# Key norms of the recurrence in one chain for four heads instead of two

## The chip, the cores and the metric

The kernel runs on one core of a Trainium2 chip. The metric is the device time of one execution in microseconds (us). TensorE (PE in the profile, PEld for its weight loads) multiplies matrices, VectorE (DVE) and ScalarE (ACT) work element by element, GpSimd (POOL) does small copies and clears, SyncE (SP) issues the transfers. Each engine runs its own instructions strictly in order; semaphores tie the engines together.

## The reference

Two layers, each a token mixer and an MLP, over a sequence of T = 256 tokens with 2048 channels. Half of the mixer is a recurrence of 16 heads with 64 channels each (RWKV-7). What the change touches is the norm of its keys:

```
heads = lambda z: z.reshape(B, T, H, N).astype(jnp.float32)
kk = heads(k * k_k)
kk = kk / jnp.maximum(jnp.sqrt(jnp.sum(kk * kk, -1, keepdims=True)), 1e-12)
k = k * (1 + (a - 1) * k_a)
```

The normalised `kk` enters the state update of every step, beside the receptance `r`, the decay, `k` and the value. The other half of the mixer is an attention of 16 heads; both halves are put together and projected by one output matrix.

## The kernel before

All activations lie with channels on the 128 partitions and the 256 tokens along the free side, so one tile [128, 256] holds two heads, and the recurrence works by such **pairs**: eight pairs per layer, in two halves of four (`half_in(0)`, `half_in(1)`). For pair `p`, `half_in` (L684) makes two blocks of the input projection, first receptance `r`, then key `k`: a block (L240) is 48 matmuls of 128x256 into one PSUM bank `acc`, from two weight units that are loaded (L220), split into a high part `wh` on ACT (L226) and a low part `wl` on DVE (L227). `ev0` (L437) evicts a block through ACT and DVE (L423, L424) into a tile `rk`, of which there are four. In the first half of layer 0 there are no such blocks: `r` and `k` come from sums that are ready before.

Then `rwkv_a` (L491) runs for the pair. It makes two small matmuls `zw`, `za` for decay and gate; from `zw` ACT and DVE make the decay products `P` and `Pi` (L501 to L506); the key's square goes to ACT (L511); `head_rsqrt` (L297) sums it per head and token with two matmuls `tp` of two columns, clamps the sums (L302, 128x4), makes the inverse root in ten DVE instructions of 128x4 (`rsqrt`, L290: one guess at L291, then three rounds of L293, L294, L295), spreads it over the 64 channels (L305, `exa`), turns it with two PE transposes (L308, `rb`) and multiplies it into the key (L514, the normalised key). With it come `bk` (L520 to L522), the two `UR` tiles (L533, L534), sixteen matmuls `mt`, their masks (L541, L542), a transpose `bkt`, `vp`, and `bonus`, whose product with the value (L565, `vt`) ends the pair. All the PSUM tiles of this, `zw`, `za`, `tp`, `rb`, `mt`, `bkt`, `vp`, `bonus`, take turns in one pool of two banks (tag `mxa`), so pairs run one behind the other. When all four pairs of a half are done, `rwkv_b` inverts 32x32 blocks in a long DVE loop, `rwkv_c` runs the state over four chunks, `rwkv_out` finishes (`half_out`). The attention that follows takes its scores (`sc`) from the same two banks.

What sets the order on an engine is a scheduler that places instructions when their inputs are due by its own estimates, earlier code first, with weight splits and evictions raised by `high_priority`. So blocks of later code (attention's inputs `cin`, `Kd`, `q`, and `va`) are laid between the steps of `rwkv_a` on PE, as filler.

Of the kernel before, what the change touches and what calls it, by code (L numbers as in the profile page):

```python
# [15 lines left out]
OP = mybir.AluOpType  # L16
# [151 lines left out]
def tile_trunk(tc, ap, outT, dbg=None):  # L168
    nc = tc.nc
    V, A, G, PE, SY = nc.vector, nc.scalar, nc.gpsimd, nc.tensor, nc.sync  # L170
    with ExitStack() as ctx:
# [4 lines left out]
                "loa": 1, "loc": 1, "sm": 1, "pc": 2, "tya": 6, "tyc": 6, "tyn": 8,}  # L176
# [16 lines left out]
        def tiny(th, n, dt=FT):  # L193
            return st("ty" + th, [128, n], dt)
# [102 lines left out]
        def head_rsqrt(th, sq, ind, floor):  # L297
            tp = mx(th, [128, 2, 2], "tp")
            for i in range(2):
                mm(tp[:, i], sq[:, i * 128:i * 128 + 128], ind)  # L300
            v, y, t = tiny(th, 4), tiny(th, 4), tiny(th, 4)
            V.tensor_scalar(v, tp.rearrange("p a b -> p (a b)"), floor, None, op0=OP.max)  # L302
            rsqrt(y, v, t)
            ex = st("ex" + th, [128, 4, 64])
            V.tensor_copy(ex, y[:, :, None].to_broadcast([128, 4, 64]))  # L305
            b = mx(th, [128, T], "rb")
            for i in range(2):
                PE.transpose(b[:, i * 128:i * 128 + 128], ex[:, 2 * i:2 * i + 2].rearrange("p a b -> p (a b)"), ident)  # L308
            return b
# [100 lines left out]
        for l in range(NL):  # L410
# [80 lines left out]
            def rwkv_a(pi, p, r, k, H):  # L491
# [18 lines left out]
                sq = st("a6", [128, T])  # L510
                A.activation(sq, k, AF.Square, scale=vc(l, "kk", pi))  # L511
                rb = head_rsqrt("a", sq, cs("hind"), 1e-24)
                kkn = st("a7", [128, T])
                V.scalar_tensor_tensor(kkn, k, vc(l, "kk", pi), rb, op0=OP.mult, op1=OP.mult)  # L514
# [9 lines left out]

                V.scalar_tensor_tensor(sq, r, vc(l, "rk", pi), kp, op0=OP.mult, op1=OP.mult)
# [156 lines left out]
            def half_in(half):  # L682
# [3 lines left out]
                for p in range(4):  # L686
                    pi = half * 4 + p
                    for i in range(2):
                        b = 12 + 2 * pi + i
                        if l > 0 or b >= NS:  # L690
                            block(win, 2 * b if half == 0 else 2 * (b + 8), hs, lambda acc: ev0(b, acc))
                        elif b >= 16:
                            ev0(b, sums[b // 2][:, b % 2])
                    rwkv_a(pi, p, rkt.pop(2 * pi), rkt.pop(2 * pi + 1), H)
# [462 lines left out]
```

## Time and profile before

| | us |
|---|---|
| three timed runs, median | 2791.06 (2787.33 to 2794.6) |
| profiled execution, its own time | 2785.48 |
| span of the profiled execution | 2783.7 |
| PE busy / PEld busy | 2657.1 / 2431.0 |
| DVE busy / ACT busy | 2084.5 / 1517.5 |

The profiled execution lies 5.6 us under the median of the runs. Matmuls are pipelined, so a PE that is always busy may still be slow; the busy time of the weight loads (PEld) is the better sign of how well PE is fed, since it fills a stretch only where matmuls follow each other without a wait. The time falls into stretches: layer 0's input start up to 204 us, its mixer up to about 660, its MLP up to 1400, then layer 1's mixer and MLP. The MLPs run at the full rate of matmuls; the mixers don't.

### The profile page before, as it was taken

The numbers are of one execution on the slowest core, as the hardware profiler recorded it, in microseconds if no ns is written. First come the engines' busy times: TensorE is split into PE (matmuls) and PEld (weight loads), VectorE is DVE, ScalarE is ACT, GpSimd is POOL, SyncE is SP. The second block draws the span as 40 slices with busy tenths as digits, with TensorE's granted clock in tenths as the row PEclk, the third lists the DMA queues.
The fourth block names the chain that finished last, engine by engine and source line by source line (L and its number), as shares of the span: only waits on it lengthen the run. The fifth ranks groups of instructions, "written<-read, shape, count | busy, mean of one in ns | idle before, by whom it ended". The sixth has DMA issues, their size and how long they took to land. (4 is left out here: it accounts for less than half of the span.)

```text
span 2783.7 us, 59154 instructions
## 1 busy us (share of the span) xinstructions
PE 2657.1 (95%) x22666; PEld 2431.0 (87%) x22666; DVE 2084.5 (75%) x4662; ACT 1517.5 (55%) x3269; POOL 69.6 (2%) x205
## 2 busy tenths in 40 slices
PE   7998899998999999999999999999999999999997
PEld 4776677746999999999999887787799999999997
DVE  3677868656789788888998786787797566666567
ACT  3345345554575554645657544556567565564655
POOL 0000010000000000000000001000000000000000
PEclk9999999998999999999999999999999999999999
DMA  9976756386579999999986444334556777776664
GB/s 312 318 260 242 248 181 202 128 259 217 178 237 365 319 342 345 338 350 333 348 264 203 148 146 133 114 107 128 169 190 197 236 224 230 232 229 205 197 194 124
DMA packets 206780, 639.75 MB, mean 230 GB/s; under 512 B 23392, under 2 KB 42848, under 8 KB 206496
## 3 DMA queue, kind: packets, MB, share of 16 engines
q1 hardware_dynamic: 206496, 635.96, 68.4%
q8 instruction: 178, 2.92, 0.4%
q14 instruction: 106, 0.87, 0.1%
HBM read 629.58 MB, written 6.29 MB: 228 GB/s over the span
## 5 line engine op out<-in xcount | busy, mean ns | idle before, releaser
L226 ACT CAST wh<-wf 128x512 fp32r<-128x512 f32 x1536 | 946.2, 620 | 845.9 <-PE acc L206 449.8
L227 DVE TENSOR_TENSOR wl<-wf,wh 128x512 fp32r<-128x512 f32 x1536 | 1037.3, 688 | 373.2 <-ACT wh L226 361.4
L206 PE MATMUL acc<-hhi,wh 128*128 128x256 f32 x3456 | 981.1, 284 | 15.4 <-ACT hhi L405 7.3
L206 PE MATMUL acc<-hhi,wl 128*128 128x256 f32 x3456 | 971.0, 281 | 8.7 <-DVE wl L227 8.6
L206 PE MATMUL acc<-hlo,wh 128*128 128x256 f32 x3456 | 968.9, 281 | 0.2 <-DVE hlo L407 0.2
L206 PE MATMUL acc<-hi,wh 128*128 128x256 f32 x2560 | 714.6, 279 | 5.8 <-DVE res L1061 3.8
L206 PE MATMUL acc<-lo,wh 128*128 128x256 f32 x2560 | 715.2, 280 | 1.3 <-DVE lo L215 1.3
L206 PE MATMUL acc<-hi,wl 128*128 128x256 f32 x2560 | 714.3, 279 | 0.0
L206 PEld LDWEIGHTS acc<-hhi,wh 128*128 128x128 f32 x3456 | 654.4, 189 | 58.9 <-issue 22.6
L206 PEld LDWEIGHTS acc<-hhi,wl 128*128 128x128 f32 x3456 | 654.5, 189 | 18.3 <-DVE wl L227 13.0
L206 PEld LDWEIGHTS acc<-hlo,wh 128*128 128x128 f32 x3456 | 653.8, 189 | 8.9 <-issue 4.7
L206 PEld LDWEIGHTS acc<-hi,wh 128*128 128x128 f32 x2560 | 484.6, 189 | 7.5 <-ACT hi L214 2.8
L206 PEld LDWEIGHTS acc<-lo,wh 128*128 128x128 f32 x2560 | 483.6, 189 | 3.5 <-DVE lo L215 2.3
L206 PEld LDWEIGHTS acc<-hi,wl 128*128 128x128 f32 x2560 | 484.4, 189 | 0.9 <-issue 0.8
L344 DVE CUSTOM_DVE_ANT_0 wa<-wa,cond,vec 128x1024 f32<-128x1024 f32 x112 | 143.2, 1278 | 0.2 <-DMA wa<-in_wada 0.2
L344 DVE CUSTOM_DVE_ANT_0 wa<-wa,cond,modh 128x1024 f32<-128x1024 f32 x112 | 143.1, 1278 | 0.0
L206 PE MATMUL gv<-wap,cT 128*32 128x512 f32 x640 | 90.4, 638 | 21.8 <-DMA wap<-in_wad 21.5
L1101 DVE TENSOR_TENSOR lo<-relu,hi 128x256 fp32r<-128x256 f32 x128 | 54.0, 425 | 45.5 <-ACT relu L1100 45.3
L288 DVE TENSOR_TENSOR sum<-sum,acc 128x512 f32<-128x512 f32 x70 | 48.0, 686 | 47.5 <-PE acc L206 47.5
L885 ACT ACTIVATE P<-P,tyn 128x128 f32<-128x128 f32 (+1 forms) x128 | 57.2, 448 | 10.3 <-DVE tyn L883 9.6
L1099 ACT ACTIVATE hi<-relu 128x256 fp32r<-128x256 f32 x128 | 53.5, 422 | 3.5
L1100 ACT ACTIVATE relu<-relu 128x256 f32<-128x256 f32 x128 | 53.3, 421 | 3.6
(290 smaller groups left out, 2329.2 us busy)
## 6 DMA issues: line engine op xcount, KB each, us to landing
wf<-in_w SPq DMA_DIRECT2D x512, 512.0 KB, 4.7
wa<-in_wada SPq DMA_DIRECT2D x224, 512.0 KB, 5.6
wf<-in_win SPq DMA_DIRECT2D x192, 512.0 KB, 3.9
wap<-in_wad SPq DMA_DIRECT2D x208, 256.0 KB, 4.7
wf<-in_wout SPq DMA_DIRECT2D x64, 512.0 KB, 3.8
wap<-in_wad SPq DMA_DIRECT2D x56, 512.0 KB, 4.7
cw<-in_cw SPq DMA_DIRECT2D x16, 512.0 KB, 4.6
xin<-in_xT SPq DMA_DIRECT2D x16, 128.0 KB, 5.9
```

The lines of the kernel that those rows point to most:

```text
L206: return PE.matmul(o, l, r, start=start, stop=stop, skip_group_check=True)
L226: A.copy(wh, wf[:, s])
L227: V.tensor_sub(wl, wf[:, s], wh.bitcast(FT))
L288: V.tensor_add(s, s, bank)
L344: V.tensor_tensor_reduce(wa, wa, cb, 0.5, init, OP.mult, OP.add, dst)
L885: A.activation(P[:, h, c:c + n], P[:, h, c:c + n], AF.Exp, bias=m[:, 2 * h + i:2 * h + i + 1], scale=-1.0, accum_out=z[:, 2 * h + i:2 * h ...
L1099: A.activation(hi, t, AF.Square)
L1100: A.activation(t, t, AF.Square)
L1101: gate[0] = V.tensor_sub(lo, t, hi.bitcast(FT)).ins
```

## The change

`head_rsqrt` and the pair's own key norm go. A new function `key_norms` makes the norms of two pairs (four heads) in one chain of small instructions, which are 128x8 instead of 128x4, and `half_in` calls it after the blocks of every second pair; then `rwkv_a` runs for both pairs, with the normalised key handed in. The tiles `a6` (square, later the bonus product) and `a7` (normalised key) get two buffers each.

```
-        def head_rsqrt(th, sq, ind, floor):
-            tp = mx(th, [128, 2, 2], "tp")
...
+        def key_norms(l, pi, ks):
+
+            tp = mx("a", [128, 2, 2, 2], "tp")
+            for q, k in enumerate(ks):
+                sq = st("a6", [128, T])
+                A.activation(sq, k, AF.Square, scale=vc(l, "kk", pi + q))
+                for i in range(2):
+                    mm(tp[:, q, i], sq[:, i * 128:i * 128 + 128], cs("hind"))
+            v, y, t = tiny("a", 8), tiny("a", 8), tiny("a", 8)
+            V.tensor_scalar(v, tp.rearrange("p q a b -> p (q a b)"), 1e-24, None, op0=OP.max)
             rsqrt(y, v, t)
...
+            out = []
+            for q, k in enumerate(ks):
+                ex = st("exa", [128, 4, 64])
+                V.tensor_copy(ex, y[:, 4 * q:4 * q + 4, None].to_broadcast([128, 4, 64]))
+                rb = mx("a", [128, T], "rb")
+                for i in range(2):
+                    PE.transpose(rb[:, i * 128:i * 128 + 128], ex[:, 2 * i:2 * i + 2].rearrange("p a b -> p (a b)"), ident)
+                out.append(st("a7", [128, T], name="kkn"))
+                V.scalar_tensor_tensor(out[-1], k, vc(l, "kk", pi + q), rb, op0=OP.mult, op1=OP.mult)
+            return out
...
-            def rwkv_a(pi, p, r, k, H):
+            def rwkv_a(pi, p, r, k, kkn, H):
...
-                sq = st("a6", [128, T])
-                A.activation(sq, k, AF.Square, scale=vc(l, "kk", pi))
-                rb = head_rsqrt("a", sq, cs("hind"), 1e-24)
-                kkn = st("a7", [128, T])
-                V.scalar_tensor_tensor(kkn, k, vc(l, "kk", pi), rb, op0=OP.mult, op1=OP.mult)
...
-                    rwkv_a(pi, p, rkt.pop(2 * pi), rkt.pop(2 * pi + 1), H)
+                    if p % 2 == 1:
+                        kkn = key_norms(l, pi - 1, [rkt[2 * pi - 1], rkt[2 * pi + 1]])
+                        for q in range(2):
+                            rwkv_a(pi - 1 + q, p - 1 + q, rkt.pop(2 * pi - 2 + 2 * q), rkt.pop(2 * pi - 1 + 2 * q), kkn[q], H)
```

Since the scheduler sets the order, the diff doesn't show where the instructions land. Two places, with the tiles' numbers. First DVE in the first half of layer 0, the end of the second pair's root before (`tya` are the small tiles, `a9` is `bk`, `a6` the bonus product, `a7` the normalised key):

```order
L522 TENSOR_TENSOR a9_2489<-kp_2486,a1_2448 128x4x64
L293 TENSOR_TENSOR tya_2467<-tya_2466 128x4
L525 SCALAR_TENSOR_TENSOR a6_2460<-rk_2301,vec0_71,kp_2486 128x256
L294 SCALAR_TENSOR_TENSOR tya_2467<-tya_2467,tya_2465 128x4
L709 TENSOR_TENSOR mod0_73<-m4_3334,vec0_71 128x4
L295 SCALAR_TENSOR_TENSOR tya_2466<-tya_2467,tya_2466 128x4
L305 COPY exa_2479<-tya_2466 128x256
L514 SCALAR_TENSOR_TENSOR a7_2484<-rk_2306,vec0_71,rb_2481 128x256
L520 SCALAR_TENSOR_TENSOR a5_2458<-a5_2458,a7_2484 128x256
```

In the changed kernel the same engine in the same half, the end of the root for the third and fourth pair (L311 spreads, L316 makes the normalised key `kkn`, L510 is the first DVE instruction of the third pair's `rwkv_a`):

```order
L293 TENSOR_TENSOR tya_2563<-tya_2562 128x8
L294 SCALAR_TENSOR_TENSOR tya_2563<-tya_2563,tya_2561 128x8
L295 SCALAR_TENSOR_TENSOR tya_2562<-tya_2563,tya_2562 128x8
L311 COPY exa_2575<-tya_2562 128x256
L316 SCALAR_TENSOR_TENSOR kkn_2580<-rk_2537,vec0_71,rb_2577 128x256
L227 TENSOR_TENSOR wl_3711<-wf_3708,wh_3710 128x512
L227 TENSOR_TENSOR wl_3715<-wf_3708,wh_3714 128x512
L311 COPY exa_2582<-tya_2562 128x256
L739 TENSOR_TENSOR rx_3699<-rx_3699,cst_63 128x256
L741 TENSOR_TENSOR rsn_3703<-acc_3622,cst_63 128x256
L316 SCALAR_TENSOR_TENSOR kkn_2587<-rk_2547,vec0_71,rb_2584 128x256
L742 TENSOR_TENSOR Kd_3621<-rx_3699,rsn_3703 128x256
```

Before, other instructions of the pair stand between the small ones; now the small ones stand one behind the other, ahead of both pairs' `rwkv_a`. Second, PE in the first half of layer 1, where before the first pair's sums `tp` come in the middle of the second pair's receptance block (`acc_20702`):

```order
L206 MATMUL acc_20702<-hhi_19331,wh_20709 128x256
L206 MATMUL acc_20702<-hhi_19331,wl_20710 128x256
L206 MATMUL tp_20619<-cst_63,a6_20617 128x2 x2
L206 MATMUL acc_20702<-hlo_19332,wh_20709 128x256
L206 MATMUL acc_20702<-hhi_19341,wh_20709 128x256
```

and now, in the changed kernel, behind the last matmul of the second pair's key block (`acc_20619`), with the third pair's receptance block (`acc_20890`) after it:

```order
L206 MATMUL acc_20619<-hhi_19379,wl_20661 128x256
L206 MATMUL acc_20619<-hlo_19380,wh_20660 128x256
L206 MATMUL tp_20693<-cst_63,a6_20694 128x2 x2
L206 MATMUL acc_20890<-hhi_19229,wh_20893 128x256
L206 MATMUL acc_20890<-hhi_19229,wl_20894 128x256
```

So the first pair's norm moved by nearly two blocks of PE work. Behind it, still in layer 1's first half, `zw` of the first pair now follows the second transpose `rb` of the chain:

```order
L206 MATMUL acc_20964<-hhi_19279,wh_20971 128x256
L314 MATMUL rb_20725<-cst_63,exa_20723 128x128 x2
L206 MATMUL zw_20734<-lx0_19942,wa2_20732 128x256
L206 MATMUL acc_20964<-hhi_19279,wl_20972 128x256
L206 MATMUL acc_20964<-hlo_19280,wh_20971 128x256
```

Before, that `zw` stood ahead of all receptance and key blocks of the half; the tiles `acc_20964` are the third pair's key block, which fills the time of the chain.

## Rows read from the trace of the kernel before

**Rows 1.** The page: the span; the busy time of each engine with its share of the span and its number of instructions; and, of the costliest groups, the weight splits on DVE (busy time, mean ns of one, then the idle time before them and what ended most of it).

```profile
span 2783.7 us, 59154 instructions
...
PE 2657.1 (95%) x22666; PEld 2431.0 (87%) x22666; DVE 2084.5 (75%) x4662; ACT 1517.5 (55%) x3269; POOL 69.6 (2%) x205
...
L227 DVE TENSOR_TENSOR wl<-wf,wh 128x512 fp32r<-128x512 f32 x1536 | 1037.3, 688 | 373.2 <-ACT wh L226 361.4
```

**Rows 2.** Busy time by stretch. The columns are named in the first line; "x" counts instructions. The stretches are, in order, layer 0's four pairs of the first half, its `rwkv_b` and `rwkv_c`, its pairs of the second half, a part of its MLP, then layer 1's pairs of the first half and of the second half, and its attention.

```profile
core 0: us, PE busy (x) PEld busy (x) DVE busy (x) ACT busy (x) POOL busy (x), PEclk, DMA share, GB/s
204.00:296.00 92.00, 83.75 (x606) 65.17 (x606) 71.65 (x199) 50.03 (x128) 8.65 (x36) 0.96 0.69 234
296.00:385.00 89.00, 81.14 (x874) 61.99 (x872) 64.48 (x170) 36.12 (x107) 10.25 (x25) 0.92 0.61 211
385.00:476.00 91.00, 86.99 (x576) 69.55 (x575) 73.05 (x198) 47.55 (x112) 3.56 (x12) 1.00 0.67 216
...
770.00:1400.00 630.00, 630.00 (x5529) 630.00 (x5529) 551.37 (x953) 363.03 (x689) 1.06 (x2) 1.00 0.92 332
1553.00:1637.00 84.00, 79.62 (x596) 72.11 (x596) 69.51 (x183) 51.43 (x122) 4.96 (x20) 1.00 0.42 132
...
1740.00:1826.00 86.00, 81.05 (x524) 68.54 (x526) 71.12 (x184) 50.54 (x119) 4.09 (x14) 1.00 0.41 123
1826.00:1990.00 164.00, 154.40 (x1471) 123.71 (x1468) 118.77 (x446) 105.39 (x316) 5.21 (x10) 0.99 0.35 106
```

**Rows 3.** The small tiles `tya` of the chain: engine, operation, count, then the shortest, median and longest duration in ns, the first and last start in us, the shape.

```profile
L293 DVE TENSOR_TENSOR tya<-tya x48: 143/156/164, 215.2 to 1798.7; 128x4 f32<-128x4 f32 x48
...
L302 DVE TENSOR_SCALAR tya<-tp x16: 148/162/164, 214.2 to 1794.3; 128x4 f32<-128x4 f32 x16
L305 DVE COPY exa<-tya x16: 279/293/296, 221.3 to 1800.4; 128x256 f32<-128x256 f32 x16
```

**Rows 4.** DVE in order of time in layer 0's first half: start and duration in us, then the instruction, and in brackets the idle time before it with what ended it. The first two rows belong to the first pair, the last three to the third, the others to the second.

```profile
214.24 0.15 DVE L302 TENSOR_SCALAR tya<-tp 128x4 f32<-128x4 f32 x1
214.31 0.40 DVE L516 TENSOR_SCALAR kp<-a,dv 128x256 f32<-128x256 f32 x1
...
235.84 0.42 DVE L565 TENSOR_TENSOR vt<-bonus,vt 128x256 f32<-128x256 f32 x1 [1.04 <-PE bonus L206]
237.44 0.29 DVE L502 TENSOR_SCALAR a<-a 128x256 f32<-128x256 f32 x1 [1.18 <-ACT a L501]
238.11 0.16 DVE L302 TENSOR_SCALAR tya<-tp 128x4 f32<-128x4 f32 x1 [0.37 <-PE tp L206]
...
242.92 0.30 DVE L305 COPY exa<-tya 128x256 f32<-128x256 f32 x1
243.75 0.48 DVE L514 SCALAR_TENSOR_TENSOR a<-rk,vec,rb 128x256 f32<-128x256 f32 x1 [0.53 <-PE rb L308]
...
256.74 0.42 DVE L565 TENSOR_TENSOR vt<-bonus,vt 128x256 f32<-128x256 f32 x1 [2.23 <-PE bonus L206]
...
259.86 0.16 DVE L293 TENSOR_TENSOR tya<-tya 128x4 f32<-128x4 f32 x1
260.06 0.16 DVE L294 SCALAR_TENSOR_TENSOR tya<-tya 128x4 f32<-128x4 f32 x1
...
276.03 0.43 DVE L565 TENSOR_TENSOR vt<-bonus,vt 128x256 f32<-128x256 f32 x1 [3.36 <-PE bonus L206]
```

**Rows 5.** PE in order of time, the same second pair of layer 0's first half and the start of the third.

```profile
236.20 0.70 PE L206 MATMUL zw<-lx,wa 96*128 96x256 f32 x2 [0.16 <-ACT SV L562]
...
237.46 0.61 PE L206 MATMUL tp<-cst,a 128*128 128x2 f32 x4
...
247.10 2.01 PE L206 MATMUL mt<-UR,a 64*128 64x128 f32 x16 [0.24 <-DVE UR L533]
...
257.10 0.70 PE L206 MATMUL zw<-lx,wa 96*128 96x256 f32 x2 [0.28 <-ACT SV L562]
```

**Rows 6.** Who waited for whom among PE's weight loads between 204 and 296 us: us in total, times, longest. One row, that of the waits for the low weights.

```profile
PEld acc L206 <- DVE wl L227: 0.5, 1, 0.5
```

**Rows 7.** DVE in order of time where blocks feed the pairs: evictions of receptance and key into `rk` (L424), the clamp at the chain's start (L302) and the end of a pair (L565). The first three rows are layer 0's second half (the second pair's key, its clamp, the last pair's end), the next two layer 1's first half (the first pair's clamp, the second pair's key), the last three layer 1's second half (the first pair's clamp, the second pair's key, the last pair's end).

```profile
389.37 0.48 DVE L424 SCALAR_TENSOR_TENSOR rk<-acc,dv,sht 128x256 f32<-128x256 f32 x1
392.63 0.15 DVE L302 TENSOR_SCALAR tya<-tp 128x4 f32<-128x4 f32 x1
...
457.11 0.42 DVE L565 TENSOR_TENSOR vt<-bonus,vt 128x256 f32<-128x256 f32 x1
...
1560.76 0.16 DVE L302 TENSOR_SCALAR tya<-tp 128x4 f32<-128x4 f32 x1 [0.46 <-PE tp L206]
...
1576.72 0.48 DVE L424 SCALAR_TENSOR_TENSOR rk<-acc,dv,sht 128x256 f32<-128x256 f32 x1
...
1726.35 0.16 DVE L302 TENSOR_SCALAR tya<-tp 128x4 f32<-128x4 f32 x1 [1.12 <-PE tp L206]
...
1743.57 0.48 DVE L424 SCALAR_TENSOR_TENSOR rk<-acc,dv,sht 128x256 f32<-128x256 f32 x1
...
1811.58 0.42 DVE L565 TENSOR_TENSOR vt<-bonus,vt 128x256 f32<-128x256 f32 x1
```

**Rows 8.** PE in order of time: the first scores of the attention in layer 0 and in layer 1.

```profile
476.60 0.60 PE L206 MATMUL cs<-kcd,q 128*128 128x32 f32 x4 [0.19 <-DVE q L735]
...
1825.00 0.63 PE L206 MATMUL cs<-kcd,q 128*128 128x32 f32 x4 [0.24 <-DVE q L735]
```

More of the change, by code (lines that the diff above doesn't have):

```diff
@@ L175, in tile_trunk @@
         BUFS = {"S": 52, "OG": 4, "wf": 5, "wh": 4, "wl": 4, "UR": 8, "TM": 8, "BK": 8, "SV": 2, "QB": 5, "ZV": 2, "Us": 2, "rk": 4, "sh": 2,
-                "loa": 1, "loc": 1, "sm": 1, "pc": 2, "tya": 6, "tyc": 6, "tyn": 8,}
+                "loa": 1, "a6": 2, "a7": 2, "loc": 1, "sm": 1, "pc": 2, "tya": 6, "tyc": 6, "tyn": 8,}
         def st(tag, shape, dt=FT, name=None):
@@ L295, in rsqrt @@
                 V.scalar_tensor_tensor(y, t, 1.5, y, op0=OP.add, op1=OP.mult)
-        def head_rsqrt(th, sq, ind, floor):
-            tp = mx(th, [128, 2, 2], "tp")
[L299 to L302, printed above, removed]
-            rsqrt(y, v, t)
[L304 to L309, printed above, removed]
+        def key_norms(l, pi, ks):
[7 more added lines that the diff above has]
+            V.tensor_scalar(v, tp.rearrange("p q a b -> p (q a b)"), 1e-24, None, op0=OP.max)
+            rsqrt(y, v, t)
+            out = []
[8 more added lines that the diff above has]
+            return out
         vecs, mods, modh = [], [], st("modh", [128, 96])
@@ L523, in rwkv_a @@
                 A.copy(bk[64:128, :, 2], bk[64:128, :, 0])
+                sq = st("a6", [128, T])
                 V.scalar_tensor_tensor(sq, r, vc(l, "rk", pi), kp, op0=OP.mult, op1=OP.mult)
```

## The prediction

> **What bounds the kernel now.** The page comes first: PE is busy for 95% of the span, PEld for 87% [rows 1]. Since a pipelined matmul counts as busy while it waits for its turn, I read PEld by stretch [rows 2]. In the MLP the weight loads fill 630 of 630 us, so nothing but matmuls sets the time there. In the mixers they fill less: 65.17 of 92 us (71%) while layer 0's first four pairs run, 69.55 of 91 (76%) for its second four, 72.11 of 84 (86%) and 68.54 of 86 (80%) for the two halves of layer 1. So in the stretches that the change touches PE stands or crawls for 29, 24, 14 and 20% of the time, and the rest is matmul work that the change leaves alone. DVE is busy for 71.65 of 92 and 71.12 of 86 us there, about four fifths: it is loaded, but not full.
>
> Why does PE stand? The pairs are a serial chain of small steps over PE, ACT and DVE. In layer 0 two pairs end 20.90 us apart (235.84 to 256.74) and the next 19.29 us later [rows 4], and each `zw` follows the end of the pair before by some 0.4 us [rows 4, 5], because they share two PSUM banks. Within the second pair, from `zw` at 236.20 to `mt` at 247.10, 10.90 us pass [rows 5]; the norm is part of that path. PE runs filler blocks meanwhile, so a microsecond off this chain isn't a microsecond off the end. It is worth what PE stood for.
>
> **The change, part by part.**
>
> *Removed instructions.* Sixteen chains become eight. Each chain has eleven small DVE instructions (the clamp, one guess, nine of three rounds), so 8 x 11 = 88 go. One takes 156 to 162 ns [rows 3]. What it costs DVE depends on its neighbours: an unrelated instruction starts 0.07 us after a clamp of 0.15 us (214.24, 214.31), while a dependent one starts 0.20 us after its forerunner (259.86, 260.06) [rows 4]. So DVE gets back 88 x 0.07 = 6.2 to 88 x 0.20 = 17.6 us. Little of it reaches PE: in layer 0's first half the weight loads waited for low weights for 0.5 us in all [rows 6]. Four such halves make 2 us at most; I take 1 us.
>
> *Wider instructions.* The chain's tiles grow from 128x4 to 128x8. Between 128x4 (156 ns) and the copy of 128x256 (293 ns) lie 137 ns for 252 columns [rows 3], or 0.5 ns a column: 88 remaining instructions by 4 columns by 0.5 ns is 0.2 us. From below the bound is nothing. Squares, sums, copies, transposes and the products with the key keep their number and shape.
>
> *Moved out of a pair: the gain.* `rwkv_a` now begins with the key ready, so between `zw` and `mt` the chain, the copy, the transpose and the product fall out of DVE's queue. That is 11 x 0.07 = 0.8 us if the small ones were woven into other work, or 11 x 0.20 = 2.2 us if they stood alone; the copy, 0.30; the idle wait for the transpose, 0.53; the product, 0.48 [rows 4]. Sum 2.1 to 3.5 us a pair. I take 3.5, since the third pair's small ones, which stand alone, are nearer to how most chains look than the second pair's. Two pairs: 7.0 us (4.2 to 7.0).
>
> *Put ahead of two pairs: the cost.* The order shows the small instructions one behind the other and `zw` behind the second transpose. So from the place where `zw` would have started: sums to clamp, 238.11 - 237.46 = 0.65 [rows 4, 5]; eleven dependent instructions, 2.2; copy to product, 243.75 - 242.92 = 0.83, and the product 0.48 [rows 4]; two weight splits that the order puts in between, 2 x 0.688 = 1.4 [rows 1]; the second copy and its transpose, 0.83. That is 6.4 us, or 5.0 where no splits lie between. I take 6.0, because the splits are there in the order. Net for two pairs: 6.0 - 7.0 = -1.0 us, with bounds 5.0 - 7.0 = -2.0 and 6.4 - 4.2 = +2.2.
>
> *The first pair of each half.* In layer 0's first half all keys come from sums, so nothing is waited for but the chain: clamp at 214.24, hence sums at 213.6, plus 6.4 to the first `zw`, plus the 20.5 us from `zw` to `vt` (236.20, 256.74) less 3.5, gives 237.0 where it was 235.84: +1.2 us. In the other three halves the first pair waits for the second pair's key block. Layer 1's first half started its clamp at 1560.76, and that key was evicted at 1576.72; its second half at 1726.35 and 1743.57 [rows 7]. PE isn't idle for that: it runs the blocks that it has to run anyway, and the attention, which needs the banks after the last pair, begins only at 476.60 and 1825.00 [rows 8] against last pairs that ended at 457.11 and 1811.58 [rows 7]. This slack of 19.5 and 13.4 us is the cover; what it costs when it is gone is the second rival.
>
> *Buffers.* The four `rk` tiles now hold two whole pairs until the first of them is through, so the third pair's receptance can be evicted only after a key of the first two was last read. That is the product with the decay gate, early in `rwkv_a`; I cost it at nothing while PE has the 48 matmuls of the next block, and the same slack covers it.
>
> *Sum.* Seven groups at -1.0 and one at +1.2 shorten the chain by 5.8 us. Weighted with the shares for which PE stood (0.29, 0.24, 0.14, 0.20, mean 0.22) that is 1.3 us. With 1 us of DVE relief and 0.2 us against it: -2.1 us on the profiled execution's 2785.48. That execution lies 5.6 us below the median, so against the median the forecast is 2791.06 - 2.1 = **2789**. What can be told from no change here is about 0.3%, or 8.4 us: this is no change that can be measured.
>
> **The rivals.**
>
> *The whole chain counts.* If the end of the mixer hangs on the pairs' chain and not on PE's work, each group pays in full, at its best bound: 7 x 2.0 = 14, less 1.2, plus the 1 us: about -14, so 2777. For it: in layer 0 PE stands for a quarter of the mixer, and rwkv_b can't start before the fourth pair. Against it: layer 1 is fed at 80 to 86%, and the first score waits for a `q` block, not for the pairs (the bracket of both rows names `q` [rows 8]).
>
> *The late first pair outruns the slack.* The place is the second half of each layer. In layer 1 the half took 1811.58 - 1726.35 = 85.2 us; started at 1744.6, behind the second key, it ends at 1829.8 without any saving, and at 1834.2 if each group costs the upper bound of +2.2; the attention would have begun at 1825.0, so 4.8 to 9.2 us are exposed. In layer 0 three pairs took 457.11 - 392.63 = 64.5 us, so four take 86.0; started at 390.4 they end at 476.4 to 480.8, against 476.6: 0 to 4.2 us. Together up to 13 us, less the 1 us of relief: 2803. It decides from the point where a group no longer gets shorter than two pairs were. For it: DVE isn't full, and the first of two pairs now waits for work that it doesn't need. Against it: PE gets the second half's blocks earlier too, as nothing of the first pair stands between them.
>
> The Trainium skill, "Perfetto Trace Analysis", section "Optimizing Scalar/DVE Operations", speaks for this rival: grouping into larger operations helps where the engine is saturated, and where it isn't but makes others wait, breaking instructions up lets work be done sooner. The trace meets the second condition, with DVE at four fifths; by that rule the time would come out at this rival's figure.
>
> *The order itself.* The scheduler lays out the rest of both mixers anew, and the mean granted clock was 0.92 in the stretch of rwkv_b and rwkv_c and 0.96 ahead of it [rows 2]: PE, which stands most there, ran part of them at 1.2 instead of 2.4 GHz. 8% of 89 us is 7 us; as much more or less at the lower level is worth that, either way, on top of the forecast: 2782 or 2796.
>
> **How the numbers follow.** Forecast, 2781 to 2797: 0.45. The whole chain, 2772 to 2781: 0.28. The late first pair, 2798 to 2806: 0.22. A reshuffle that carries it past 0.3%: 0.05, half to each side. The range that leaves out 2 in 10 reaches to most of both rivals, 2773 to 2803. Faster by over 0.3% (below 2782.7): the first rival, half of the last case and a tail of the forecast, 0.31. Slower (above 2799.4): the second rival and the other half, 0.24. Within: 0.45.
>
> **What would show it.** In the profile of the changed kernel: 88 fewer DVE instructions and 6 to 18 us less DVE busy time; `zw` to `mt` at 7 to 8 us instead of 10.9; 5 to 6.5 us between the end of every second pair and the next `zw`; groups of two pairs 1 us shorter. First scores within 5 us of where they were, waiting for `q`. The forecast is wrong if `sc` waits for the banks of the pairs, if PEld's share in the pairs' stretches moves by more than three points, or if groups shrink by over 3 us and the attention moves with them.

## The result and the profile after

The change made the kernel slower: 2814.63 us median of seven runs (2800.68 to 2820.83) against 2789.55 us (2786.18 to 2794.6) for the kernel before, a ratio of 1.0077 with a 95% interval of 1.006 to 1.0094. The forecast was 2789, its range ended at 2803; the sign and the size were wrong. The profiled executions differ by more than the medians, 2814.63 against 2785.48; the one of before ran at a mean granted clock of 0.984, and its runs beside the experiments had a median of 0.98. The seven runs of the kernel before lie 8.4 us apart, so a difference of some 8 us between two single executions proves nothing here; verdicts come from the medians, places from the traces.

The page of the changed kernel, lines as in [rows 1]:

```profile
span 2812.9 us, 59102 instructions
...
PE 2675.6 (95%) x22666; PEld 2447.3 (87%) x22666; DVE 2079.8 (74%) x4574; ACT 1519.5 (54%) x3269; POOL 69.7 (2%) x205
...
L227 DVE TENSOR_TENSOR wl<-wf,wh 128x512 fp32r<-128x512 f32 x1536 | 1038.3, 689 | 389.6 <-ACT wh L226 378.6
```

DVE lost its 88 instructions and only 4.7 us of busy time; PE has the same 22666 matmuls and is busy for 18.5 us more.

The small tiles (lines as in [rows 3]), 10 ns longer at twice the width:

```profile
L293 DVE TENSOR_TENSOR tya<-tya x24: 157/166/169, 214.2 to 1801.9; 128x8 f32<-128x8 f32 x24
...
L306 DVE TENSOR_SCALAR tya<-tp x8: 166/167/169, 212.6 to 1799.2; 128x8 f32<-128x8 f32 x8
```

PE and then DVE in order of time, first half of layer 0, answering to [rows 5] and [rows 4] (L306 is now the clamp, L569 the end of a pair):

```profile
212.04 0.50 PE L206 MATMUL tp<-cst,a 128*128 128x2 f32 x4
...
219.84 1.06 PE L206 MATMUL zw<-lx,wa 96*128 96x256 f32 x2
...
227.71 1.16 PE L206 MATMUL mt<-UR,a 64*128 64x128 f32 x8
...
237.94 0.70 PE L206 MATMUL zw<-lx,wa 96*128 96x256 f32 x2 [0.33 <-ACT SV L566]
...
244.49 1.16 PE L206 MATMUL mt<-UR,a 64*128 64x128 f32 x8 [0.16 <-DVE a L524]
```

```profile
237.36 0.42 DVE L569 TENSOR_TENSOR vt<-bonus,vt 128x256 f32<-128x256 f32 x1
...
255.14 0.42 DVE L569 TENSOR_TENSOR vt<-bonus,vt 128x256 f32<-128x256 f32 x1 [1.01 <-PE bonus L206]
...
291.18 0.42 DVE L569 TENSOR_TENSOR vt<-bonus,vt 128x256 f32<-128x256 f32 x1 [0.24 <-PE bonus L206]
```

Where nothing is waited for, the forecast's chain is there: `zw` to `mt` takes 7.87 and 6.55 us where it took 10.90, the chain starts 7.8 us ahead of the first `zw`, the first group ends at 237.36 (the forecast had 237.0), and the half ends no later than before (291.18), where that row stood at

```profile
295.16 0.42 DVE L565 TENSOR_TENSOR vt<-bonus,vt 128x256 f32<-128x256 f32 x1 [1.29 <-PE bonus L206]
```

The same where blocks feed the pairs, DVE, answering to [rows 7]. The first three rows are layer 0's second half (clamp, end of the first pair, of the last), the next five layer 1's first half (key of the second pair, clamp, end of the first pair, `Mu`, the first instruction of `rwkv_b`, end of the last pair), the last three its second half (clamp, ends of the first and the last pair):

```profile
388.44 0.17 DVE L306 TENSOR_SCALAR tya<-tp 128x8 f32<-128x8 f32 x1 [0.88 <-PE tp L206]
...
416.65 0.42 DVE L569 TENSOR_TENSOR vt<-bonus,vt 128x256 f32<-128x256 f32 x1 [1.84 <-PE bonus L206]
...
474.65 0.42 DVE L569 TENSOR_TENSOR vt<-bonus,vt 128x256 f32<-128x256 f32 x1 [0.25 <-PE bonus L206]
...
1580.20 0.48 DVE L432 SCALAR_TENSOR_TENSOR rk<-acc,dv,sht 128x256 f32<-128x256 f32 x1
...
1582.53 0.17 DVE L306 TENSOR_SCALAR tya<-tp 128x8 f32<-128x8 f32 x1 [0.38 <-PE tp L206]
...
1604.29 0.42 DVE L569 TENSOR_TENSOR vt<-bonus,vt 128x256 f32<-128x256 f32 x1 [2.56 <-PE bonus L206]
...
1664.99 1.25 DVE L574 STREAM_TRANSPOSE Mu<-Dt 128x1024 f32<-128x1024 f32 x1 [0.99 <-ACT Dt L549]
1666.26 0.43 DVE L569 TENSOR_TENSOR vt<-bonus,vt 128x256 f32<-128x256 f32 x1
...
1737.75 0.17 DVE L306 TENSOR_SCALAR tya<-tp 128x8 f32<-128x8 f32 x1 [6.87 <-PE tp L206]
...
1774.75 0.42 DVE L569 TENSOR_TENSOR vt<-bonus,vt 128x256 f32<-128x256 f32 x1
...
1836.24 0.42 DVE L569 TENSOR_TENSOR vt<-bonus,vt 128x256 f32<-128x256 f32 x1 [0.94 <-PE bonus L206]
```

The first pairs of these three halves ended before at

```profile
385.20 0.42 DVE L565 TENSOR_TENSOR vt<-bonus,vt 128x256 f32<-128x256 f32 x1 [1.21 <-PE bonus L206]
...
1577.12 0.41 DVE L565 TENSOR_TENSOR vt<-bonus,vt 128x256 f32<-128x256 f32 x1
...
1750.76 0.42 DVE L565 TENSOR_TENSOR vt<-bonus,vt 128x256 f32<-128x256 f32 x1 [0.61 <-PE bonus L206]
```

Layer 1 as a whole starts 10.4 us later (its last value block is evicted at 1547.7, before at 1537.3). Beyond that, the first half's first pair ends 16.8 us later and its last 19.5; of the second half 13.6 and 14.3. In layer 0's second half it is 31.5 and 17.5. The `Mu` row is the one to see: it stands ahead of the last pair's `vt`. It stood so before too:

```profile
1635.06 1.25 DVE L570 STREAM_TRANSPOSE Mu<-Dt 128x1024 f32<-128x1024 f32 x1
1636.34 0.42 DVE L565 TENSOR_TENSOR vt<-bonus,vt 128x256 f32<-128x256 f32 x1
```

So `rwkv_b` takes over from the last pair at once; in the kernel before, its `Mu` started 1.3 to 4.4 us ahead of the last pair's end in all four halves. There is no slack on that side. The attention's first scores, the successor that the forecast looked at [rows 8], moved by 6.3 us in layer 0 and by 17.7, of which 10.4 are the late start, in layer 1, where the forecast allowed 5 (PE in order of time):

```profile
482.93 0.60 PE L206 MATMUL cs<-kcd,q 128*128 128x32 f32 x4 [0.52 <-DVE q L742]
...
1842.67 0.63 PE L206 MATMUL cs<-kcd,q 128*128 128x32 f32 x4
```

**Where the time went.** Busy time by stretch in layer 1, columns as in [rows 2]: from the last value block to the end of the first half's last pair, on to the end of the second half's, and on to the end of the mixer. The kernel before:

```profile
1537.30:1636.30 99.00, 94.60 (x675) 82.40 (x674) 78.31 (x203) 57.05 (x133) 4.64 (x20) 1.00 0.43 133
1636.30:1811.60 175.30, 162.83 (x1451) 139.39 (x1450) 136.28 (x353) 86.36 (x216) 14.42 (x39) 0.99 0.44 135
1811.60:2055.90 244.30, 231.72 (x2088) 198.81 (x2087) 191.99 (x608) 145.86 (x394) 5.81 (x12) 0.99 0.47 149
```

The changed kernel:

```profile
1547.70:1666.30 118.60, 112.89 (x817) 100.89 (x817) 89.07 (x204) 65.56 (x151) 4.58 (x21) 0.99 0.44 138
1666.30:1836.20 169.90, 159.76 (x1345) 137.83 (x1344) 127.69 (x311) 82.75 (x210) 13.81 (x37) 0.92 0.40 126
1836.20:2085.60 249.40, 232.05 (x2053) 198.71 (x2052) 189.14 (x606) 143.58 (x386) 6.01 (x13) 0.95 0.44 142
```

The first stretch is 19.6 us longer, and PE uses it: 142 matmuls more, as the forecast said. The two stretches behind it have 3398 matmuls where they had 3539, and take 419.3 us where they took 419.6. By these two executions alone the filler that ran early brings nothing back later. But the clock differs, 0.92 and 0.95 for 0.99, and the last experiment has a kernel in which no norm moved, with nearly the same matmuls in these stretches as before (second and third stretch):

```profile
1642.10:1817.90 175.80, 163.16 (x1450) 139.82 (x1449) 136.43 (x352) 86.40 (x216) 14.36 (x38) 0.99 0.42 134
1817.90:2070.40 252.50, 238.04 (x2089) 204.35 (x2087) 192.64 (x608) 146.09 (x394) 5.82 (x12) 0.95 0.45 144
```

Its third stretch ran at 0.95 and took 8.2 us more than that of before at 0.99 (0.04 x 252.5 = 10). So the change's 249.4 us at 0.95 needn't be its own doing, and against this kernel its two later stretches are 9.0 us shorter (419.3 for 428.3): part of the filler's time does come back. The same shows in layer 0, its second half and then the rest of its mixer. The kernel before:

```profile
295.20:457.10 161.90, 150.08 (x1341) 115.86 (x1340) 120.03 (x324) 73.57 (x197) 13.19 (x36) 0.96 0.65 219
457.10:752.90 295.80, 274.22 (x2302) 217.27 (x2300) 197.47 (x621) 158.52 (x422) 6.27 (x14) 0.94 0.61 196
```

The changed kernel:

```profile
291.20:474.60 183.40, 170.88 (x1416) 131.41 (x1415) 125.32 (x312) 81.22 (x213) 14.55 (x38) 0.94 0.61 206
474.60:761.10 286.50, 257.47 (x2248) 202.57 (x2246) 190.31 (x614) 153.09 (x411) 6.54 (x14) 0.97 0.61 194
```

The half is 21.5 us longer, and 9.3 us of that come back behind it; from its last value block to its end layer 0's mixer became 10.4 us longer (543 to 553).

The clock in layer 1's second stretch, 20 us each, and under it the only wait of 2 us or more of PE between 1715 and 1745 us (total, times, longest):

```profile
1700.00:1720.00 20.00, 17.15 (x145) 16.45 (x144) 18.98 (x47) 11.74 (x28) 0.60 (x4) 1.00 0.67 220
1720.00:1740.00 20.00, 19.32 (x202) 17.89 (x203) 4.89 (x13) 5.52 (x16) 0.10 (x1) 0.50 0.19 54
```

```profile
PE hp L206 <- DVE O L594: 2.7, 1, 2.7
```

In these 20 us PE ran at 1.2 GHz throughout. Just before, it had run 145 matmuls in 20 us, and it stood 2.7 us for a transpose in `rwkv_b` where the clock fell.

### The profile page after: what moved, and what is told of

Same layout as the page of the kernel before. It is cut to its first block, busy times and chain, and to the rows that moved or that the text cites. A ratio compares the mean times of both kernels' runs of the same rounds, so it can differ in the third digit from the quotient of the medians.

```text
span 2812.9 us, 59102 instructions
## 1 busy us (share of the span) xinstructions
PE 2675.6 (95%) x22666; PEld 2447.3 (87%) x22666; DVE 2079.8 (74%) x4574; ACT 1519.5 (54%) x3269; POOL 69.7 (2%) x205
```

## The experiments

Times of the kernel before beside these runs had medians of 2792.88 to 2795.5. "Lateness" is that of the last pair of layer 1's first half against the kernel before, counted from the last value block.

### The change in one half alone

Four kernels: the change made in one of the four halves (the condition names it), the other three with one norm per pair in its old place.

```
-                    if p % 2 == 1:
+                    if not (l == 0 and half == 0):
+                        rwkv_a(pi, p, rkt.pop(2 * pi), rkt.pop(2 * pi + 1), None, H)
+                    elif p % 2 == 1:
...
+                if kkn is None:
+                    kkn = key_norms(l, pi, [k])[0]
```

Layer 0's first half, where no block is waited for:

> Four heads in one chain only in layer 0's first half, where receptance and key come from sums that are ready; the other three halves make one norm per pair inside rwkv_a as before. Late-pair theory (the loss comes from first pairs that wait for the second pair's key block, and runs on through rwkv_b and rwkv_c into the next half): no wait for a block here, so -3 to +3 us against the kernel before. Straight-chain theory (eleven small instructions one behind the other, ahead of zw, cost by themselves): +5 us, a quarter of the whole loss. Clock theory (any new order moves PE's stretches at the lower clock): anything within 10 us, and as much as the mean granted clock says.

Layer 1's first half:

> Four heads in one chain only in layer 1's first half. Late-pair theory: most of the loss, +12 to +20 us, with the last pair of this half ending about 20 us later against the start of the layer, and rwkv_c behind it. Straight-chain theory: +5 us. Clock theory: the loss comes and goes with a stretch at 1.2 GHz near rwkv_b.

Layer 1's second half:

> Four heads in one chain only in layer 1's second half. Late-pair theory: the pairs end later but within the slack before the attention, 0 to +6 us. Straight-chain theory: +5 us.

Layer 0's second half:

> Four heads in one chain only in layer 0's second half. Late-pair theory: 0 to +6 us, since the first pair was held by rwkv_c of the first half anyway. Straight-chain theory: +5 us. If the four halves add up to the whole change (+25 us), the halves act by themselves; if not, they act on each other.

Measured: 1.0007 [0.9989, 1.0024] in the half without blocks; 1.0035 [1.002, 1.005], 1.0044 [1.0025, 1.0064] and 1.0049 [1.0031, 1.0067] in the three with blocks. In the last three the pairs of that half end later (first and last by 16.8 and 19.6, 16.9 and 12.0, 27.3 and 17.7 us) and no others ahead of it; in the first none of that half moves by more than 3.1 us. So where no block is waited for the chain of merged norms costs nothing that can be told, and each half that is fed by blocks costs 10 to 14 us; for the two second halves that is above the 0 to 6 us expected. Lateness of 12 us in layer 1's second half, which the forecast saw inside its slack of 13.4, went with a mixer that was 17.6 us longer in layer 1; the kernel of the last experiment, without any late pair, shows 8.6 there. The three don't add: 1.28% together against 0.77%. With the first half of layer 1 alone changed, the second half's pairs were already 5 to 14 us late, so its own wait had room there.

### What makes the pairs late

Two separate chains of 128x4 for two pairs, in the place of the change:

```
-                        kkn = key_norms(l, pi - 1, [rkt[2 * pi - 1], rkt[2 * pi + 1]])
+                        kkn = key_norms(l, pi - 1, [rkt[2 * pi - 1]]) + key_norms(l, pi, [rkt[2 * pi + 1]])
```

> Everything as in the change (the norms of two pairs behind all four of their blocks, ahead of both pairs), but each pair's norm is a chain of its own with 128x4 tiles, as before: 176 small instructions again, only the merging is undone. Late first pair: the loss stays, ratio to the kernel before 1.006 to 1.012 (+17 to +33 us); first clamps of layer 1's halves at about 1580 and 1737 us. If the width or the length of the merged chain were the cost: at least half of the loss goes, below 1.004. Order or clock alone: any value between 0.998 and 1.008.

1.0064 [1.0043, 1.0084]. The loss stays; the merging itself is worth nothing that can be told. The first clamps came at 1569.2 and 1717.0 us, earlier than expected; the last pair of layer 1's first half still ended 27.2 us late.

One norm per pair, ahead of its `zw`, no wait for a second pair:

```
-                    if p % 2 == 1:
-                        kkn = key_norms(l, pi - 1, [rkt[2 * pi - 1], rkt[2 * pi + 1]])
...
+                    kkn = key_norms(l, pi, [rkt[2 * pi + 1]])
+                    rwkv_a(pi, p, rkt.pop(2 * pi), rkt.pop(2 * pi + 1), kkn[0], H)
```

> One norm per pair, made in a chain of its own ahead of the pair's zw as in the change, but right behind the pair's own key block: nothing waits for a second pair. 176 small instructions. Late first pair: most of the loss goes, 0.998 to 1.003 (-6 to +8 us), first clamps of layer 1's halves within 3 us of 1561 and 1726. Straight chain (a norm that stands ahead of zw instead of inside the pair lengthens every pair by its own length): 16 pairs, 4 to 6 us each, weighed with the share for which PE stands, +10 to +20 us: 1.004 to 1.007, with pairs 3 us or more further apart than before.

1.0072 [1.0057, 1.0087]: the late-pair expectation fell, the other one's upper end was met. This has sixteen chains ahead of a `zw` where the change has eight, so it isn't a part of the change's cost alone. PE in order of time in layer 1's first half, first pair:

```profile
1571.47 0.61 PE L206 MATMUL tp<-cst,a 128*128 128x2 f32 x4
...
1576.06 0.60 PE L206 MATMUL zw<-lx,wa 96*128 96x256 f32 x2
```

In the kernel before, that `zw` stood at

```profile
1513.53 0.70 PE L206 MATMUL zw<-lx,wa 96*128 96x256 f32 x2 [0.21 <-ACT lx L461]
```

The decay part needs no key, and ran 47 us ahead of the clamp [rows 7]; with the norm in front of it, it waits for the key block and the whole chain. The pairs of this half then end 21.0, 24.5 and 23.1 us apart where it had been 19.4, 19.2 and 20.6, and the lateness is 13.1. Of the 3 us or more by which the second theory had every pair further apart, one of these three gaps shows it.

The reverse, the wait alone: the old norm inside its pair, the work of both pairs behind the blocks of both (`None` has the pair make its own norm).

```
-                    rwkv_a(pi, p, rkt.pop(2 * pi), rkt.pop(2 * pi + 1), H)
+                    for q in (-1, 0) if p % 2 == 1 else ():
+                        rwkv_a(pi + q, p + q, rkt.pop(2 * pi + 2 * q), rkt.pop(2 * pi + 2 * q + 1), None, H)
```

> The kernel before with its 16 norms, each inside its pair behind zw, but the work of both pairs is placed behind the blocks of both, as in the change. So the first pair of each two waits for the second pair's key block and nothing else is changed; the decay part (zw) of each half's first pair still runs early. If the wait is what costs (late first pair): 1.004 to 1.009, last pairs of layer 1's halves 12 us or more later. If zw behind the norm is what costs (the norm, and with it the key block, ahead of the decay part that needs no key): 0.999 to 1.003, pairs about 20 us apart as before and the half no more than 8 us later at its end.

1.0067 [1.0043, 1.0091]. `zw` stands at 1530.20 there, early, as before; DVE shows the first pair's clamp only at the second pair's key, and the lateness is 12.4 (in layer 1's second half 7.0, where 12 or more was expected):

```profile
1586.03 0.16 DVE L307 TENSOR_SCALAR tya<-tp 128x4 f32<-128x4 f32 x1 [0.79 <-PE tp L206]
1586.70 0.48 DVE L433 SCALAR_TENSOR_TENSOR rk<-acc,dv,sht 128x256 f32<-128x256 f32 x1
...
1603.35 0.42 DVE L572 TENSOR_TENSOR vt<-bonus,vt 128x256 f32<-128x256 f32 x1 [2.29 <-PE bonus L206]
```

So there are two delays, and kernels that have either alone lose as much as the change. Three versions take away part of them. Key blocks of both pairs ahead of both receptance blocks:

```
-                    for i in range(2):
-                        b = 12 + 2 * pi + i
+                    for pj, i in (((pi, 1), (pi + 1, 1), (pi, 0), (pi + 1, 0)) if p % 2 == 0 else ()):
+                        b = 12 + 2 * pj + i
```

> The change with its merged chains, but the blocks of two pairs are made in the order key, key, receptance, receptance, so that the chain starts after two blocks instead of four and runs beside the receptance blocks. Late first pair: the norm is ready by the time the first receptance block is done, but the first pair still waits for its receptance, the third block instead of the second: the first pair is late by one block (about 10 us) instead of two, half of the loss goes: 1.000 to 1.005 (0 to +14 us). Straight chain: all of the loss goes, since the chain is hidden behind two blocks, and 88 small instructions fewer stay: 0.997 to 1.000.

1.0058 [1.0041, 1.0075], lateness 17.6 where 10 was expected; both ranges were missed. The decay part of the first of two pairs ahead of the merged chain (the first pair's `kkn()` makes both norms, behind `zw`, `za` and the decay products):

```
+                if callable(kkn):
+                    kkn = kkn()
```

> The change with its merged chains behind both blocks, but the decay part of the first of two pairs (zw, za and what ACT and DVE make of them) is issued ahead of the merged chain instead of behind it. The wait for the second key stays, the chain no longer stands between the keys and zw for the first pair. Wait alone: as the change, 1.005 to 1.010. zw behind the norm alone: most of the loss goes, 0.998 to 1.003. Both of about equal weight: 1.003 to 1.006.

1.0086 [1.0067, 1.0106], lateness 9.7. Both together:

> As the run before it, and the four blocks in the order key, key, receptance, receptance: the merged chain runs beside the first receptance block with the decay part done. The first pair still waits one block longer than in the kernel before. Wait alone: half of the change's loss, 1.002 to 1.005. zw behind the norm alone: no loss and the 88 instructions saved, 0.994 to 1.000.

1.0053 [1.0033, 1.0072], lateness 9.1. None gets out of the loss, and it doesn't grow with the lateness: 9.1, 9.7, 12.4, 13.1, 17.6, 19.5 (the change) and 27.2 us (two chains) went with 1.0053, 1.0086, 1.0067, 1.0072, 1.0058, 1.0077 and 1.0064. But lateness is counted from layer 1's last value block and leaves out what was lost ahead of it. That block came 14.1, 21.6, 16.7, 11.3, 14.5, 10.4 and 0.3 us later than before (1537.31), in the same order; here in the second and in the last kernel:

```profile
1558.91 0.48 DVE L433 SCALAR_TENSOR_TENSOR vT<-acc,dv,sht 128x256 f32<-128x256 f32 x1
```

```profile
1537.58 0.48 DVE L433 SCALAR_TENSOR_TENSOR vT<-acc,dv,sht 128x256 f32<-128x256 f32 x1
```

Both together make 23 to 32 us in all seven, by one execution each. The ten kernels in which a half fed by blocks ends 9 us or more late, with PE's work and the `wf` tiles as they were, lie at 1.0035 to 1.0086; the six without such a half, at 0.995 to 1.0015.

### Receptance tiles

> The change with eight rk tiles instead of four, so that no receptance or key waits for a tile of the pairs before; the weights' wf tiles are four instead of five to make room, and the next run has that alone. If the tiles held by two pairs cost: the ratio is 0.003 or more below the next run's, and last pairs of the halves 5 us or more earlier. If they cost nothing, as the prediction took it: within 0.002 of the next run.

> The change with four wf tiles instead of five, the control for the run before it. All theories: as the change or slightly slower, 1.007 to 1.015.

The edits are two numbers, `"rk": 8` and `"wf": 4`. Measured 1.0157 [1.0134, 1.0179] and, for the control, 1.018 [1.0156, 1.0203]. With eight tiles it takes 0.23% less, between the two expectations, and the intervals overlap: the tiles aren't what most of the 0.77% is made of. The control, above its range, shows what a fifth `wf` tile is worth here: without it the change's ratio is 1.018 instead of 1.0077.

### Chain or matmuls

Two rounds of the inverse root left out of the kernel before (`for _ in range(1)` in the key norm's chain):

> The kernel before with one round instead of three in the key norm's inverse root (the last two rounds are left out): 6 small DVE instructions fewer in each of the 16 pairs, 96 in all. Nothing else is changed. If the pairs' chain sets the end of the mixers: 6 x 0.20 = 1.2 us a pair, 4.8 us a half, that is passed on to the end: 0.993 to 0.997. If PE's work sets it, as the prediction weighed it (0.22 of 19 us, and 1 us for DVE): 0.997 to 1.000.

0.9955 [0.994, 0.9971]: 0.0045 x 2795.5 = 12.6 us for 16 x 1.2 = 19.2 us of chain. In the profiled execution layer 1's last pairs end 4.2 and 6.0 us earlier. In layer 0 the first half is 13.0 us shorter, and the second gives 10.9 of that back.

A third of the matmuls left out of twelve of layer 1's filler blocks, in the kernel before:

```
-            mm(o, wl, xh, False, False)
-            mm(o, wh, xl, False, last)
+            mm(o, wl, xh, False, last and two)
+            if not two:
+                mm(o, wh, xl, False, last)
...
-                block(win, u, hs, lambda acc, rp: rope(acc, rp, q), True)
+                block(win, u, hs, lambda acc, rp: rope(acc, rp, q), True, two=l == 1)
```

> The kernel before with one of three matmuls (high weights by low activations) left out in twelve blocks of layer 1, the attention's inputs cin, Kd and q, which fill PE beside the recurrence: 192 matmuls of 128x256 fewer, at one each 0.115 us (the MLP's pace) 22 us of PE work. The pairs' chain is untouched. If PE's work sets the end of the mixer: 0.992 to 0.994 (-18 to -22 us). If the chain of pairs, rwkv_b, rwkv_c and heads sets it: 0.998 to 1.001, with more of PE idle or at the lower clock.

1.0018 [1.0003, 1.0033], above both ranges: 22 us less for PE, and no gain. The three stretches of layer 1:

```profile
1542.20:1651.00 108.80, 102.98 (x746) 90.70 (x745) 88.14 (x221) 64.60 (x147) 4.91 (x21) 1.00 0.49 146
1651.00:1828.30 177.30, 165.79 (x1443) 142.45 (x1442) 139.66 (x358) 89.49 (x224) 14.04 (x38) 0.97 0.44 141
1828.30:2069.60 241.30, 216.85 (x1833) 177.82 (x1832) 177.47 (x586) 136.72 (x370) 5.35 (x11) 0.89 0.43 134
```

The third has 255 matmuls fewer than before, 29 us at the MLP's 630 / 5529 = 0.114 us [rows 2], and is 3.0 us shorter; weight loads fill 74% of it instead of 81%, at a clock of 0.89 instead of 0.99. The difference in clock is worth up to 0.10 x 241.3 = 24 us, most of the 29. So the run doesn't show that PE's work counts for nothing: the lower clock can have taken the gain. The order came out otherwise too: the last pair of the first half ended 9.7 us late.

### Faster versions, and the layout

The key block of a pair ahead of its receptance, in the kernel before (`for i in (1, 0)`):

> The kernel before, one norm per pair inside the pair, but with each pair's key block ahead of its receptance block, so that the norm can run beside the receptance block. No merging. Late first pair: the first pair ends no later than before, and earlier by up to the chain's 4 to 6 us where the pair's own work was waiting for the norm: 0.995 to 1.001 (-14 to +3 us). Straight chain: the same sign, the full 8 halves' pairs gain 4 us each weighed with 0.2, -10 us. Order or clock alone: within 0.3 per cent of 1.

0.995 [0.9932, 0.9968], 2780.64 us: the fastest of all. In layer 0's second half the last pair ends 6.0 us earlier, in layer 1's halves 0.6 and 4.1.

The same with the merged chains in layer 0's first half alone:

> The key block ahead of the receptance block of the same pair, as in the run that gave 0.995, and the merged chains in the first half of layer 0 alone, where no block is waited for. Merging there alone gave 1.0007. If the effects add: 0.995 to 0.997. If the merge is worth its DVE instructions once nothing waits: 0.992 to 0.995.

0.997 [0.9957, 0.9983]: the merge, which brings the second buffers of `a6` and `a7` with it, adds nothing.

The same (without the merge) with two rounds of the root:

> Each pair's key block ahead of its receptance block (the run that gave 0.995), and two rounds instead of three in the key norm's inverse root: three small DVE instructions fewer in each pair's chain. All else is as in the kernel before. If the pairs' chain sets the mixers' length and what stands ahead of it is hidden: the norm now runs beside the receptance block, so three instructions less are worth less than half of what six gave (0.9955), 0.991 to 0.995. If the chain of small instructions were still in line with the pair: 0.990 to 0.993. If the gain of the key-first order was chance: 0.997 to 0.999.

1.001 [0.9994, 1.0027]. A miss: the two gains don't add. Layer 1's last pairs ended where they did before (0.0 and 0.1 us, so up to 4 us later than in the key-first kernel), at a median clock of 0.9765 where the key-first kernel had 0.985.

The kernel before with only the second buffers of `a6` and `a7`, no norm moved:

> The kernel before with its 16 norms in their pairs, and only the two buffers each for the square and the normalised key taken from the change; the code that makes a norm is the change's function, called for one pair inside the pair. No wait and no place of a norm is changed on purpose. If only late pairs cost: 0.998 to 1.002. What it differs from 1 beyond that is what a new layout of the instructions alone does, and is to be allowed for in the other runs: 0.995 to 1.005.

1.0015 [1.0002, 1.0029]. Layer 1's pairs end within 0.4 us of before. The layout alone can be worth 0.15%. Whether the 0.6% between the two key-first kernels is layout as well isn't shown.

## Why the prediction was wrong

*Removed instructions, wider instructions*: right in count (88), smaller in busy time (4.7 us, forecast 6 to 18); one instruction of 128x8 takes 10 ns more, 0.9 us for 88, where 0.2 was taken. They don't matter: the kernels with 176 and 88 small instructions in the change's place gave 1.0064 and 1.0077, and the merge alone, where nothing is waited for, 1.0007.

*Moved out of a pair, put ahead of two pairs*: right in kind where the half has no blocks. The second group of layer 0 takes 255.14 to 291.18, 36.0 us, where it took 38.4: 2.4 shorter, against -1.0 (-2.0 to +2.2). The second groups of the other halves are 1.6 and 1.8 us shorter and, in layer 1's first half, 4.4 longer. The chain ahead of `zw` was under-sized, 5.8 to 10.8 us from the sums to `zw` in the eight groups for 6.0, and between the end of a second pair and the next `zw` 8.0 to 11.5 us passed where 5 to 6.5 was forecast. But the same sum was used for all groups, as if a pair began with `zw` everywhere. In the halves with blocks the first `zw` had run long before the key; there the chain ahead of it is an addition, not an exchange. The run with single norms ahead of `zw` shows what that can cost: 1.0072, with twice as many chains.

*The first pair of each half* is the step that failed. It saw the wait for the second key, with the right rows, and priced it at nothing, since "this slack of 19.5 and 13.4 us is the cover". The slack was measured to the first score of the attention. The pairs' next consumer is `rwkv_b`, which starts 1.3 us ahead of the last pair's end [the `Mu` rows above], so no cover exists on that side. Each half with blocks, changed alone, cost 10 to 14 us; the wait alone, without any merged chain, 1.0067.

*Sum* left the term out with it. What a microsecond of chain is worth was weighted with 0.22, the share for which PE stood; that this was too low isn't shown cleanly. When the chain was shortened, 12.6 of 19.2 us came back, a weight of 0.66, but half as much of the same cut made the key-first kernel slower. With 22 us of PE's work gone nothing was gained, but the clock fell. These are single kernels beside a layout effect of 0.15% or more; whether the chain of pairs or PE's work sets the mixers' length more stays open.

*Buffers*: at nothing; the run with eight tiles, 0.23% under its control with overlapping intervals, leaves room for little more.

*The rivals.* "The late first pair outruns the slack" had the mechanism and the sign and was given 0.22. Its place (the second halves) was too narrow, as layer 1's first half alone cost 1.0035, and its price counted only what passes the slack: 2803 instead of 2815. The rule of the Trainium skill that spoke for it ("Perfetto Trace Analysis", "Optimizing Scalar/DVE Operations") agrees with these runs in direction only: grouping lost 0.77% where DVE was four fifths busy and others waited. But the loss doesn't come from the larger instructions, since it stays with two chains of the old width (1.0064) and is absent where no block is waited for (1.0007). "The whole chain counts" had the better weight and the wrong sign. "The order itself" may be real in size: kernels without late pairs lie between 0.995 and 1.0015.

**What stays open.** Why the three halves alone make 1.28% and the change 0.77%, and why kernels with either delay alone lose as much as the change. A part is the clock: the change's runs had a median of 0.977, those of before 0.98, at most 0.003 x 2815 = 8 of the 25 us, and in the two profiled executions (0.984 and 0.976) up to 0.008 x 2813 = 22 of 29. Whether the lower clock lengthens the mixer or only fills time in which PE would have stood differs by stretch. In the third of layer 1 the kernel with only the buffers took 8.2 us more at 0.95 for the same matmuls. In the second the run with the wait alone was as long (169.7 us) at 0.99 as the change's at 0.92 (169.9).

## What to carry to other kernels

Before a wait is costed at nothing, take the slack to the nearest consumer of everything that it delays, not to the next use of a shared resource. Grouping two independent units behind the inputs of both makes the first wait for the second, and a common step that is moved to the front also holds back the parts that never needed it; both cost more here than the instructions saved. Filler that covers a wait is borrowed from later: see by how much the stretch that it came from gets shorter, against a kernel that ran there at the same clock.

## What was not expected of the hardware

PE busy time rose by 18.5 us with the same 22666 matmuls: in 20 us of layer 1 PE ran wholly at 1.2 GHz, with 202 matmuls and weight loads busy for 17.89 us, so that it looks well fed there. Taking matmuls away lowered the clock (0.99 to 0.89 in the third stretch of layer 1) and took nearly nothing off the time. In that stretch the kernel before and the one with only the second buffers ran the same matmuls at 0.99 and 0.95, and the time differed by 8.2 us. And the two key-first kernels, with three and two rounds, had median clocks of 0.985 and 0.9765; 0.0085 x 2790 = 24 us at most, more than the 17 us between their medians, though the pairs of the one with three rounds ended up to 5 us earlier too.
